# A unit of seven products and the plain unit beside it, matmul by matmul in turn

## The chip, the core and the metric

The kernel runs on one core of one Trainium2 chip. The metric is device time in microseconds, the median of several executions. Engines are named as in the profile: PE is TensorE (matmuls), PEld its loads of the stationary operand, ACT is ScalarE, DVE is VectorE, POOL is GpSimd, SP is SyncE, which issues the DMAs.

## What is computed

Two pre-norm residual layers of a decoder trunk, for 256 tokens of width 2048 in float32. Layer 0 mixes tokens with stick-breaking attention, layer 1 with a gated delta rule. Each is followed by a dense SwiGLU FFN with a hidden width of 5632:

```python
for i in range(DEPTH):
    h = rms_norm(x, mix_norm[i])
    y = stick_breaking_mixer(h, ...) if i == 0 else gated_deltanet_mixer(h, ...)
    x = x + y
    x = x + swiglu(rms_norm(x, ffn_norm[i]), ffn_w_gu[i], ffn_w_down[i])

def swiglu(h, w_gu, w_down):
    gate, up = jnp.split(h @ w_gu, 2, axis=-1)
    return (jax.nn.silu(gate) * up) @ w_down
```

The change concerns the FFNs alone.

## The kernel before

**Products.** A float32 product is made of three products of `fp32r` operands. Each operand is split into a high and a low part, and high x high, high x low and low x high are added up in PSUM. The activations are split once, when they are made. The weights come raw from memory and are split as they arrive: `convert` (L515) has ScalarE write the high part (`act`, L307) and VectorE the low part, the raw value minus the high one (`tt`, L311).

**Blocks and units.** A block is a product of all 256 tokens with 512 columns of a weight matrix. It is cut into units of two slices of 128 rows of the weights (`UK = 2`), and a unit is the step of the main loop. There are three lanes, each with its own buffers:

- a: outside the FFNs' middle; four pairs of high and low buffers.
- b: a plain unit inside the FFN. Two slices, two halves of the tokens and three products make 12 matmuls with 512 moving columns. Two raw buffers, two pairs of high and low buffers.
- s: a unit of seven products, for six of the eleven column blocks of gate and up. A product of 2 x 2 blocks is made with seven multiplications in place of eight, so there are 7 x 3 = 21 matmuls with 256 moving columns (`seven_products`, L582). The sums of weights that it needs are made first by VectorE (`sums`, L500: three operations), then converted: high part 128x1792, low part in one or two pieces. Two or three raw buffers, two pairs of high and low buffers.

A unit's high and low buffer goes back to its lane after its last matmul; its raw buffer goes back after its low part is made.

**The order of the work.** The kernel writes every engine's instructions itself, in one program order, with a small model of the engines' times (`spend`, L288). `ffn_units` (L821) and `merge` (L868) lay out the order of the s and b units: at most two s in a row, about 1.3 b to one s. A run of three or four b is common where a block of each ends.

`stream` (L620) goes through the units one by one. In each round it issues loads (`pump`, L477, on SP's queue), makes the sums of the s units up to three places on, and converts units while `ahead < i + AHEAD`, with `AHEAD = 3`, that is up to two places on. Then it writes the unit's matmuls (`product`, L543). Between groups of three matmuls `tick` (L267) lets waiting tasks go one step: evacuations of finished blocks (`quarters`, L1002, and others), transposes of hidden activations, norms. Their matmuls go into the same TensorE queue, their other steps into ScalarE's and VectorE's. An engine carries out its queue in program order.

Of the kernel before, what the change touches and what calls it, by code (L numbers as in the profile page):

```python
# [145 lines left out]
class Trunk:  # L146
# [393 lines left out]
        quarters = lambda *w: [q for a in w for q in self.cut(a, 256)]  # L540
        u.conv = (quarters(hi), quarters(*lo), end + HOP) if u.lane == "s" else (hi, lo[0], end + HOP)

    def product(self, u):  # L543
        b, (hi, lo, after) = u.block, u.conv
        ks = range(u.k0, u.k0 + u.nk)
        if b.kind == "ba":
            acc = b.acc[0]
            c = b.cols
            for k in ks:
                o = b.ops[k]  # L550
                wh, wl = hi[:, k * c:(k + 1) * c], lo[:, k * c:(k + 1) * c]
                for j, (w, x) in enumerate(((wh, o.hi), (wh, o.lo), (wl, o.hi))):
                    self.mm(acc[:c, :S], w, x, start=k == 0 and j == 0, stop=k == len(ks) - 1 and j == 2, after=after)
        elif b.kind == "seven":
            self.seven_products(u, hi, lo, after)
        else:
            for j, k in enumerate(ks):
                o = b.ops[k]
                if not o.ready:
                    self.until(lambda: o.ready, ("operand", b.name, k))  # L560
                self.tick()
                wh, wl = hi[:, j * NB:(j + 1) * NB], lo[:, j * NB:(j + 1) * NB]
                for t in range(NT):
                    if t:
                        self.tick()
                    a, sl = b.acc[t], slice(t * P, (t + 1) * P)
                    self.mm(a, o.hi[:, sl], wh, start=u.first and j == 0, stop=False, after=after)
                    self.mm(a, o.hi[:, sl], wl, start=False, stop=False)
                    self.mm(a, o.lo[:, sl], wh, start=False, stop=u.last and j == u.nk - 1)
                o.uses -= 1  # L570
                if o.uses == 0 and o.release:
                    o.release()
        u.done = True
        if u.lane == "a":
            self.freed.append(self.t["pe"])
        else:
            u.hibuf.t = self.t["pe"]
            self.lanes[u.lane][1].put(u.hibuf)
        if u.leaves:
            self.leave_b()  # L580

    def seven_products(self, u, hi, lo, after):  # L582


        b = u.block
        o = b.ops[u.k0 // 2]
        if not o.ready:
            self.until(lambda: o.ready, ("forms", b.name, u.k0))
        x = o.parts()

        for p, w, bank, half in ((1, 0, 1, 0), (2, 2, 0, 0), (4, 6, 3, 1), (3, 1, 3, 0), (5, 3, 2, 0), (7, 4, 2, 1), (6, 5, 0, 1)):
            self.tick()
            xh, xl = x[p - 1]
            a = b.acc[bank][:, 256 * half:256 * (half + 1)]
            self.mm(a, xh, hi[w], start=u.first and p in (1, 2, 4, 5), stop=False, after=after)
            self.mm(a, xh, lo[w], start=False, stop=False)
            self.mm(a, xl, hi[w], start=False, stop=u.last and p in (1, 6, 3, 7))
        o.uses -= 1

    def begin(self, b):  # L600
# [19 lines left out]
    def stream(self, units):  # L620
        self.units, self.at, self.freed, self.owner, self.more = units, 0, [], [None, None], None
        for i, u in enumerate(units):
            u.idx = i
            u.block.name = getattr(u.block, "name", i)
        for i in range(self.RAW):
            if i % 2 == 0:
                self.load_x(i // 2)
            self.load(units[i])
        self.load_x(3)
        self.spawn(self.more_constants(), "constants")  # L630
        ahead = 1
        self.convert(units[0])
        self.until(lambda: units[0].block.ops[0].ready, "first operand")
        for i, u in enumerate(units):
            self.at, spins = i, 0
            self.pump()
            while True:
                for v in units[i:i + self.AHEAD + 1]:
                    if v.lane == "s" and not v.summed:
                        if not v.loaded:  # L640
                            break
                        self.sums(v)
                while ahead < min(i + self.AHEAD, len(units)) and self.may_convert(units[ahead]):
                    self.convert(units[ahead])
                    ahead += 1
                    self.pump()
                if ahead > i:
                    break
                spins += 1
                assert spins < 100, ("conversion", u.block.name, u.lane, u.loaded)  # L650
                self.until(lambda: self.may_load(u) or u.loaded, ("load", u.block.name))
                self.pump()
            if u.first:
                self.begin(u.block)
            self.product(u)
            if u.last:
                b = u.block
                b.evacuated = False
                self.spawn(self.after_block(b), f"block {b.name}", front=True).urgent = True
        self.until(lambda: not self.tasks, "end")  # L660

    def load_x(self, n):

        self.nc.sync.dma_start(self.xs[n], self.ins["x"][0, :, n * NB:(n + 1) * NB].rearrange("(t p) d -> p t d", p=P))
        task = self.spawn(self.norm_part(self.norms[0], n), f"norm {n}")
        task.base = task.ready = self.transfer(P * NT * NB * 4, 0.0)
# [986 lines left out]
```

## Time and profile before

| | |
|---|---|
| median of 3 runs | 2745.24 us (2743.29 to 2746.49) |
| the profiled execution's own time | 2744.59 us |
| its span, first to last instruction | 2742.9 us |
| granted TensorE clock, mean | 0.998 |
| PE, PEld busy | 2706.2, 2305.9 us |
| DVE, ACT busy | 2169.5, 1489.6 us |
| read from HBM | 489.33 MB |
| units: lane a, b, s | 461, 260, 192 |
| stretches with s units | about 455 to 1052 and 2049 to 2645 us |

The page gives busy times and the busy share in 40 slices. The timeline lists instructions in order of time, with equal neighbours merged into one row (x2, x9): start, duration, engine, line, operation, `out<-in`, and in brackets the idle time before it with the engine that ended it. A matmul's duration in the rows is its way through the array, longer than the distance to the next start; that distance is its price. The windows view gives busy time by engine in a stretch, then the granted clock, the DMA share and GB/s. In the rows, b's raw and converted weights are `slab` and `slabs`, those of lanes s and a are `w`. Matmuls of s units have 256 moving columns and read `w`; those of b units have 512 and read `slabs`.

### The profile page before, as it was taken

Reading aid. Unit: us, or ns where it says so; the run is one execution under the profiler, and the core shown is the slowest. Engines: PE = TensorE matmul, PEld = TensorE weight load, DVE = VectorE, ACT = ScalarE, POOL = GpSimd, SP = SyncE. Lnnn points to the kernel's source line nnn. Section 1 sums busy time; section 2 is a strip of 40 time slices with the busy share of each in tenths; the row PEclk is TensorE's granted clock in tenths of the full one; section 3 lists DMA queues with packets and bytes.
Section 4 is the critical chain, followed back from the end, with each engine's and each line's share of the span. In section 5 each row is a group of like instructions: output and inputs, shape, how many; then the busy total and the mean of one; then the engine's idle time right before and its main releaser. Section 6 shows DMA issues by size and latency. Waiting matters only on the chain.

```text
span 2742.9 us, 39666 instructions
## 1 busy us (share of the span) xinstructions
PE 2706.2 (99%) x15018; PEld 2305.9 (84%) x15018; DVE 2169.5 (79%) x3378; ACT 1489.6 (54%) x1968; POOL 11.2 (0%) x95
## 2 busy tenths in 40 slices
PE   7999999999999999999999999999999999999999
PEld 6888888889888888888888888888878888888887
DVE  5555567899999897668878877987678899998975
ACT  5555555545554554555666556655565455455553
POOL 0000000000000000000000000000000000000000
PEclk9999999999999999999999999999999999999999
DMA  6555555656656656556655556556555566656564
GB/s 202 161 168 166 179 176 171 192 177 204 196 185 198 200 178 207 175 172 186 173 154 180 174 150 179 165 159 186 154 177 191 185 196 196 191 185 203 181 211 158
DMA packets 299835, 496.65 MB, mean 181 GB/s; under 512 B 37176, under 2 KB 79483, under 8 KB 299643
## 3 DMA queue, kind: packets, MB, share of 16 engines
q1 hardware_dynamic: 299594, 494.10, 57.8%
q8 instruction: 117, 1.92, 0.3%
q14 instruction: 76, 0.61, 0.1%
q10 hardware_dynamic: 48, 0.02, 0.0%
HBM read 489.33 MB, written 4.72 MB: 180 GB/s over the span
## 4 chain that ended last, share of the span: by engine, by line
PE 78%; DVE 14%; ACT 3%; issue 2%; DMA 2%; SPq 0%; ACTq 0%; DVEq 0%
PE acc L330 65%; PE bank L330 12%; DVE w L311 9%; DVE slabs L311 3%; PE bank L339 2%; ACT w L307 2%; DMA slab<-in_ffn_w_down_dram 1%; DVE slab L311 1%; DVE x L311 1%; ACT slab L307 0%; DMA slab<-in_ffn_w_gu_dram 0%; DVE slab L315 0%; DVE hTl L315 0%; DMA x<-in_x_dram 0%; ACT hTh L307 0%
## 5 line engine op out<-in xcount | busy, mean ns | idle before, releaser
L311 DVE TENSOR_TENSOR w<-w,w 128x1024 fp32r<-128x1024 f32 (+1 forms) x749 | 949.7, 1289 | 301.9 <-ACT w L307 297.3
L307 ACT ACTIVATE w<-w 128x1024 fp32r<-128x1024 f32 (+1 forms) x653 | 804.4, 1244 | 475.9 <-PE acc L330 272.5
L330 PE MATMUL acc<-w,hTh 128*128 128x512 f32 (+1 forms) x3296 | 948.6, 371 | 13.1 <-DVE w L311 7.9
L330 PEld LDWEIGHTS acc<-w,hTh 128*128 128x128 f32 x3296 | 594.4, 189 | 120.9 <-DVE w L311 12.9
L330 PE MATMUL acc<-w,hTl 128*128 128x512 f32 (+1 forms) x1648 | 603.8, 366 | 0.0
L307 ACT ACTIVATE slabs<-slab 128x1024 fp32r<-128x1024 f32 x260 | 272.3, 1052 | 320.4 <-PE acc L330 215.1
L311 DVE TENSOR_TENSOR slabs<-slab,slabs 128x1024 fp32r<-128x1024 f32 x260 | 315.6, 1219 | 68.7 <-ACT slabs L307 68.4
L330 PE MATMUL acc<-w,kh 128*128 128x512 f32 x1152 | 361.2, 395 | 0.0
L330 PEld LDWEIGHTS acc<-w,hTl 128*128 128x128 f32 x1648 | 311.5, 189 | 51.2
L330 PE MATMUL acc<-slabs,kh 128*128 128x512 f32 x1024 | 322.8, 394 | 5.9 <-DVE slabs L311 4.5
L330 PE MATMUL acc<-slabs,hTh 128*128 128x512 f32 x1056 | 328.1, 392 | 0.0
L311 DVE TENSOR_TENSOR w<-w 128x256 f32<-128x256 f32 (+1 forms) x576 | 293.7, 511 | 13.3
L330 PEld LDWEIGHTS acc<-w,kh 128*128 128x128 f32 x1152 | 211.6, 188 | 41.3
L330 PEld LDWEIGHTS acc<-slabs,kh 128*128 128x128 f32 x1024 | 187.6, 188 | 49.5 <-DVE slabs L311 11.8
L330 PEld LDWEIGHTS acc<-slabs,hTh 128*128 128x128 f32 x1056 | 193.4, 188 | 37.5 <-DVE slabs L311 1.1
L330 PE MATMUL acc<-w,kl 128*128 128x512 f32 x576 | 224.7, 390 | 0.0
L330 PE MATMUL acc<-slabs,hTl 128*128 128x512 f32 x528 | 205.6, 389 | 0.0
L330 PE MATMUL acc<-slabs,kl 128*128 128x512 f32 x512 | 199.7, 390 | 0.0
L330 PE MATMUL bank<-w,wide 128*128 128x256 f32 x1296 | 180.1, 284 | 0.0
L330 PEld LDWEIGHTS bank<-w,wide 128*128 128x128 f32 x1296 | 165.9, 192 | 0.0
L330 PEld LDWEIGHTS acc<-w,kl 128*128 128x128 f32 x576 | 108.1, 188 | 23.0
L330 PEld LDWEIGHTS acc<-slabs,hTl 128*128 128x128 f32 x528 | 99.2, 188 | 21.2
(203 smaller groups left out, 2378.1 us busy)
## 6 DMA issues: line engine op xcount, KB each, us to landing
w<-in_ffn_w_gu_dram SPq DMA_DIRECT2D x220, 512.0 KB, 4.1
slab<-in_ffn_w_gu_dram SPq DMA_DIRECT2D x132, 512.0 KB, 3.5
w<-in_gdn_w_in_dram SPq DMA_DIRECT2D x129, 512.0 KB, 3.9
slab<-in_ffn_w_down_dram SPq DMA_DIRECT2D x128, 512.0 KB, 4.4
w<-in_sb_w_in_dram SPq DMA_DIRECT2D x96, 512.0 KB, 3.6
w<-in_gdn_w_in_dram SPq DMA_DIRECT2D x128, 256.0 KB, 3.0
w<-in_gdn_w_out_dram SPq DMA_DIRECT2D x64, 512.0 KB, 3.8
w<-in_ffn_w_down_dram SPq DMA_DIRECT2D x48, 512.0 KB, 4.2
```

Source lines behind the costliest of these rows:

```text
L307: self.nc.scalar.activation(out, in_, func, **kw)
L311: self.nc.vector.tensor_tensor(out, a, b, op=op)
L330: self.nc.tensor.matmul(out, lhsT, rhs, start=start, stop=stop, skip_group_check=True)
L339: self.nc.tensor.transpose(out, in_, self.ident[:p, :p])
```

## The change

Two neighbouring units of which one is of lane s and the other of lane b are written together, unless the first ends its block or the second begins one. `product` becomes a generator, `products`, that stops after every matmul of an s or b unit, and `stream` takes one matmul from each of the two in turn until both are finished. The two must both be converted before the first matmul is written, and the loop then moves on by two units. `AHEAD` stays 3 and is counted from the first of the two. All other pairs of neighbours go as before. No instruction is added or removed; the tasks' `tick` calls stay where they are within each unit.

```diff
@@ seven_products and the plain branch of products, after each matmul
                     self.mm(a, o.hi[:, sl], wh, start=u.first and j == 0, stop=False, after=after)
+                    yield
                     self.mm(a, o.hi[:, sl], wl, start=False, stop=False)
+                    yield
                     self.mm(a, o.lo[:, sl], wh, start=False, stop=u.last and j == u.nk - 1)
+                    yield
@@ stream
-        for i, u in enumerate(units):
+        i = 0
+        while i < len(units):
+            u = units[i]
             self.at, spins = i, 0
+            both = self.together(*units[i:i + 2])
             self.pump()
...
-                if ahead > i:
+                if ahead > i + both:
                     break
                 spins += 1
                 assert spins < 100, ("conversion", u.block.name, u.lane, u.loaded)
-                self.until(lambda: self.may_load(u) or u.loaded, ("load", u.block.name))
+                v = units[ahead]
+                self.until(lambda: self.may_load(v) or v.loaded, ("load", u.block.name))
                 self.pump()
             if u.first:
                 self.begin(u.block)
-            self.product(u)
-            if u.last:
-                b = u.block
-                b.evacuated = False
-                self.spawn(self.after_block(b), f"block {b.name}", front=True).urgent = True
+            going = deque(self.products(v) for v in units[i:i + 1 + both])
+            while going:
+                try:
+                    next(going[0])
+                    going.rotate(-1)
+                except StopIteration:
+                    going.popleft()
+            for u in units[i:i + 1 + both]:
+                if u.last:
+                    b = u.block
+                    b.evacuated = False
+                    self.spawn(self.after_block(b), f"block {b.name}", front=True).urgent = True
+            i += 1 + both
+
+    def together(self, u, v=None):
+        return v is not None and {u.lane, v.lane} == {"s", "b"} and not u.last and not v.first
```

More of the change, by code (lines that the diff above doesn't have):

```diff
@@ L541, in convert, with products @@
         u.conv = (quarters(hi), quarters(*lo), end + HOP) if u.lane == "s" else (hi, lo[0], end + HOP)
-    def product(self, u):
+    def products(self, u):
         b, (hi, lo, after) = u.block, u.conv
@@ L554, in product @@
         elif b.kind == "seven":
-            self.seven_products(u, hi, lo, after)
+            yield from self.seven_products(u, hi, lo, after)
         else:
@@ L595, in seven_products @@
             self.mm(a, xh, hi[w], start=u.first and p in (1, 2, 4, 5), stop=False, after=after)
+            yield
             self.mm(a, xh, lo[w], start=False, stop=False)
+            yield
             self.mm(a, xl, hi[w], start=False, stop=u.last and p in (1, 6, 3, 7))
+            yield
         o.uses -= 1
```

## The prediction

> **What bounds the kernel now.** I read the page first (span, busy times, slices), then the windows of the two stretches that hold the units of seven products, then the waits of TensorE in them.
>
> ```profile
> span 2742.9 us, 39666 instructions
> ...
> PE 2706.2 (99%) x15018; PEld 2305.9 (84%) x15018; DVE 2169.5 (79%) x3378; ACT 1489.6 (54%) x1968; POOL 11.2 (0%) x95
> ...
> DVE  5555567899999897668878877987678899998975
> ```
>
> TensorE is the bound over the whole, and VectorE reaches nine tenths in slices 8 to 15 and again near the end. Those are the FFN stretches:
>
> ```profile
> 455.00:1052.00 597.00, 590.30 (x3543) 523.66 (x3542) 538.84 (x662) 308.54 (x268) 0.00 (x0) 1.00 0.60 192
> 2049.00:2645.00 596.00, 589.35 (x3539) 523.13 (x3538) 538.44 (x661) 307.68 (x267) 0.00 (x0) 1.00 0.60 192
> ```
>
> Columns are length, then busy time of PE, PEld, DVE, ACT, POOL. VectorE is busy for 90% of a stretch in which TensorE leaves only 6.7 us open. So two engines are nearly full, and the conversions on VectorE arrive just in time. What TensorE waited for in the first of the two:
>
> ```profile
> PE acc L330 <- DVE w L311: 3.7, 8, 0.9
> PE acc L330 <- DVE slabs L311: 2.2, 3, 1.4
> PE acc L330 <- ACT w L307: 0.6, 2, 0.4
> ```
>
> Thirteen waits, 6.5 us; the second stretch is alike. Today lateness costs almost nothing, because each unit is needed only when the one before it is finished.
>
> **How much of the kernel the change reaches.** From the units in their order, `together` takes neighbours of lanes s and b unless the first ends or the second begins a block. I wrote out that order: 82 pairs come of it (41 in each FFN; 66 with b first, 16 with s first), of 192 s units. 22 of the 82 follow directly on another pair. No instruction is added or removed; a pair is still 21 matmuls of 256 columns and 12 of 512. The first 24 of the 33 now alternate and the last nine are of 256.
>
> **The pace of alternating matmuls.** This is TensorE around one pair in its old order, s at 715.58 and b at 718.09:
>
> ```profile
> 714.22 0.62 PE L330 MATMUL acc<-slabs,kh 128*128 128x512 f32 x2
> 714.90 0.62 PE L330 MATMUL acc<-slabs,kh 128*128 128x512 f32 x2
> 715.35 0.39 PE L330 MATMUL acc<-slabs,kl 128*128 128x512 f32 x1
> 715.58 0.40 PE L330 MATMUL acc<-w,hTh 128*128 128x256 f32 x2
> 715.81 0.28 PE L330 MATMUL acc<-w,hTl 128*128 128x256 f32 x1
> 716.65 1.24 PE L330 MATMUL bank<-w,wide 128*128 128x256 f32 x9
> 717.73 0.52 PE L330 MATMUL acc<-w,wide 128*128 128x256 f32 x3
> 718.09 0.63 PE L330 MATMUL acc<-slabs,kh 128*128 128x512 f32 x2
> 718.56 0.39 PE L330 MATMUL acc<-slabs,kl 128*128 128x512 f32 x1
> ```
>
> The duration column holds the way through the array; the price of one is the distance between starts. Three of 512 columns from 714.22 to 714.90 make 0.227 each; nine of 256 from 716.65 to 717.73 make 0.120. Both are 13 ns above their columns at 2.4 per ns (213 and 107), so the extra is the same for either size. At the changes: the first two of 256 after a 512 take 715.81 - 715.58 = 0.23, 0.01 less than two steady ones; the first two of 512 after a 256 take 718.56 - 718.09 = 0.47, 0.016 more than two steady ones. The trace has no strict alternation, so I bound it. In the worst case each 512 behaves like the first two here (0.235) and each 256 gains nothing: 0.008 x 12 x 82 = +8 us. In the best case each 256 behaves as one that follows a 512 (the whole 0.01 falls on the first, 0.110) and the 512 loses nothing: -0.010 x 12 x 82 = -10 us. Added together the two observed ends nearly cancel (-0.01 and +0.016 per change), so I take 0.
>
> The Trainium skill, page "TensorE: Matmul & The Clock Gate", gives for the load of 128 stationary columns (section "LDWEIGHTS (loading the stationary operand)") 128/1.2 = 107 ns, and says in "Back-to-back issue gap" that both the load and the matmul set the spacing, with 256/2.4 + 2.5 = 109 ns for a matmul by itself. By that page a 256 run stands at its load's limit, a load would hide behind a 512, and 11 ns of 984 matmuls would go: an estimate of -11 us. The rows above speak against it: the 512s, long enough to hide any load, carry the same 13 ns.
>
> **What moves: when the second unit is needed.** TensorE starts its matmuls in the order of the code (the rows above), and the second matmul of the pair now belongs to the second unit. Its converted weights are needed 0.1 to 0.2 us after the first unit starts, not after that unit's 2.52 us (21 x 0.120) or 2.72 us (12 x 0.227). For the pair above:
>
> ```profile
> 714.12 1.05 ACT L307 ACTIVATE slabs<-slab 128x1024 fp32r<-128x1024 f32 x1
> 714.97 1.60 DVE L311 TENSOR_TENSOR w<-w 128x512 f32<-128x512 f32 x3
> 716.49 1.22 DVE L311 TENSOR_TENSOR slabs<-slab,slabs 128x1024 fp32r<-128x1024 f32 x1
> ```
>
> ScalarE has the high part of b at 715.17; VectorE first makes the sums of a later s unit and ends b's low part at 717.71. That is 2.13 us after s started and 0.38 before b needed it. In the new order TensorE stands for those 2.1 us, and its whole queue stands with it: the rest of the pair, the transposes and small products of the tasks that tick between, and through them ScalarE's evacuations. Reading all 82 pairs in this way (end of the second unit's last low part minus start of the first unit), the lateness is positive in every one: 0.10 to 3.90, mean 1.88, sum 154 us. The first and the last pair (0.10, the first of two low parts at 1.22 ending 460.88 against 460.78; and 2637.41 against 2636.46, 0.95):
>
> ```profile
> 460.78 0.40 PE L330 MATMUL acc<-w,hTh 128*128 128x256 f32 x2
> 459.66 2.35 DVE L311 TENSOR_TENSOR slabs<-slab,slabs 128x1024 fp32r<-128x1024 f32 x2
> 2636.46 0.63 PE L330 MATMUL acc<-slabs,hTh 128*128 128x512 f32 x2
> 2635.31 2.10 DVE L311 TENSOR_TENSOR w<-w,w 128x768 fp32r<-128x768 f32 x2 [0.64 <-ACT w L307]
> ```
>
> Not all of the 154 us is paid. Where VectorE's work runs on without a break, a wait of TensorE in one pair puts VectorE that much ahead for the next. Where a conversion has to wait for a buffer that TensorE gives back, the lead is lost. I followed each second unit's conversion back, operation by operation, to the matmul that released it, and took off the waits that earlier pairs had put in since. An example of a release:
>
> ```profile
> 480.38 1.06 ACT L307 ACTIVATE slabs<-slab 128x1024 fp32r<-128x1024 f32 x1 [0.80 <-PE acc L330]
> 481.34 1.69 ACT L307 ACTIVATE w<-w 128x1792 fp32r<-128x1792 f32 x1
> 483.06 2.03 DVE L311 TENSOR_TENSOR w<-w,w 128x1792 fp32r<-128x1792 f32 x1 [0.37 <-ACT w L307]
> 482.90 0.61 PE L330 MATMUL acc<-slabs,hTh 128*128 128x512 f32 x2
> ```
>
> The b lane has two pairs of high and low buffers, so the third b in a row converts only when the first is done (480.38); the s behind it is ready at 485.09, 2.19 after its partner b started at 482.90, and pays all of it. The two pairs right behind it have the same release and pay little. In all, 33 pairs pay 1.9 on average, 62 us, and the other 49 together 3: **+65 us**. Bounds: 154 if no lead is ever kept, 33 if half of these waits are covered as well.
>
> **Pairs right behind a pair.** `ahead` looks three units on from the first of a pair, so the second unit of the following pair is converted only in the following round, one unit later in the code than now. These are the durations that then stand in one line:
>
> ```profile
> L311 DVE TENSOR_TENSOR w<-w,w 128x1792 fp32r<-128x1792 f32 x144 | 196.4, 1398 | 22.3 <-ACT w L307 22.0
> L307 ACT ACTIVATE slabs<-slab 128x1024 fp32r<-128x1024 f32 x124 | 129.9, 1052 | 146.8 <-PE acc L330 87.5 <-DMA slab<-in_ffn_w_down_dram 34.4 <-DMA slab<-in_ffn_w_gu_dram 15.4
> L311 DVE TENSOR_TENSOR slabs<-slab,slabs 128x1024 fp32r<-128x1024 f32 x124 | 150.5, 1219 | 30.2 <-ACT slabs L307 30.1
> L311 DVE TENSOR_TENSOR w<-w 128x256 f32<-128x256 f32 (+1 forms) x282 | 143.9, 511 | 6.5
> ```
>
> High part of b 1.05, its low part 1.22, three sums of s 1.53, low parts of s 196.4/96 = 2.05: 5.85 us from the buffer's release, against 12 x 0.347 + 9 x 0.120 = 5.24 us of matmuls. That is 0.6 short before any hand-over between engines (the idle column gives 0.24 for one from ScalarE to VectorE). Also b's buffer comes free after 12 x 0.347 = 4.2 us and no longer after 2.7. I take 1.0 for each of the 22: **+22 us** (0 if the lead covers it, 45 at 2.05, a whole low part).
>
> **What is given back.** Of the 13 us that TensorE waits today in both stretches, some are absorbed by the new waits: **-6 us** (0 to -13). The raw loads are issued from the same queue in the same order, one round later behind a pair; loads wait for buffers that VectorE frees, so this adds nothing that isn't in VectorE's line above.
>
> **Clock.** One long wait lowers the granted clock (the figure after POOL):
>
> ```profile
> 43.00:46.00 3.00, 0.61 (x2) 0.54 (x3) 2.38 (x6) 1.36 (x3) 0.00 (x0) 0.50 0.85 283
> 46.00:50.00 4.00, 4.00 (x14) 3.12 (x13) 1.24 (x2) 0.00 (x0) 0.00 (x0) 0.55 0.48 146
> 2154.00:2157.00 3.00, 1.53 (x7) 0.98 (x6) 2.93 (x5) 2.44 (x3) 0.00 (x0) 1.00 0.00 0
> ```
>
> The 5 us wait before 45.39 brought it to 0.55 for the next 4 us, which costs 1.8; 1.5 us open near 2155 left it at 1.00. Most new waits are nearer to the latter, so 0 in the sum; four that are above 3 us could add 7. The skill's page named above, section "Why this matters for your kernels", puts the limit at idle gaps of about 3 us, which these rows allow.
>
> **Sum.** Against the profiled execution's own 2744.59 us (the span and 1.7 around it; the median of the runs is 0.65 above it): 0 + 65 + 22 - 6 = +81, so 2826 us. Low: 33 + 0 - 13 = +20, 2765. High: 154 + 22 - 6 = +170, 2915.
>
> **Rivals.**
> - *The lead is kept everywhere (no change).* If VectorE, once put ahead, stayed ahead, one wait of at most 3.9 us per FFN would do, less 6 given back: 2744.6 + 7.8 - 6 = 2746. For: it has 10% free. Against: the buffer releases above, which recur in each run of three b. Chance 0.07.
> - *Faster.* The new waits are covered and each 256 in turn sheds its 0.010: -10 us, 2735. It decides if the second unit is ready at the start in at least 70 of the 82 pairs, so that fewer than 10 us are lost. Against: 0 of 82 are ready in the trace. Chance 0.08. (By the page's load limit, weighed above, it would be -11 and 2734.)
> - *No lead is kept and clock drops join.* 154 + 45 + 7: about 2950. Chance 0.05.
> - *The forecast,* waits of 20 to 170 us: 0.80.
>
> A measurement of this kernel tells 0.2% (5.5 us) from no change. With the two slower cases: slower 0.85, within 0.2% 0.07, faster 0.08. The range 2765 to 2915 leaves out 0.2.
>
> **What would show it.** In the new profile TensorE's waits for VectorE ("w" and "slabs") should grow from 13 us to about 90 and its busy time in the two stretches stay near 1180 us, with the stretches longer by about 40 each; VectorE's share there falls from 90% to about 85%; the time outside stays within 2 us. Starts in a pair should lie 0.347 us apart from one 512 to the next. I am wrong if the waits stay under 20 us, or if 512 to 512 is off 0.347 by more than 0.01.

## The result, and the profile after

The changed kernel takes 2841.98 us (median of 5 runs, 2831.57 to 2843.57) against 2745.24 (5 runs of before): the ratio is 1.0345, with a 95% interval of 1.0334 to 1.0357. The prediction was 2826, slower.

The page's span and busy times, then the windows of the two FFN stretches (from the first unit before them to the last matmul; length, PE, PEld, DVE, ACT, POOL, clock, DMA share, GB/s):

```profile
span 2840.3 us, 39668 instructions
...
PE 2737.0 (96%) x15018; PEld 2318.2 (82%) x15018; DVE 2172.7 (76%) x3378; ACT 1489.4 (52%) x1968; POOL 11.3 (0%) x95
```

```profile
452.90:1109.50 656.60, 617.07 (x3601) 539.82 (x3600) 546.89 (x668) 312.39 (x272) 0.00 (x0) 0.98 0.56 176
2094.70:2749.60 654.90, 614.38 (x3601) 537.69 (x3600) 547.00 (x668) 312.21 (x272) 0.00 (x0) 0.99 0.56 176
```

The same units of the kernel before:

```profile
452.80:1059.30 606.50, 599.80 (x3602) 532.29 (x3601) 545.22 (x668) 312.64 (x272) 0.00 (x0) 1.00 0.60 191
2046.00:2652.20 606.20, 599.55 (x3601) 532.36 (x3600) 545.21 (x668) 312.58 (x272) 0.00 (x0) 1.00 0.60 191
```

The stretches are longer by 50.1 and 48.7 us; all the rest went from 1530.2 to 1528.8. VectorE and ScalarE do the same work as before (547 and 312 us) in more time. So nothing was added: TensorE stands. Its waits on conversions, over the whole span:

```profile
PE acc L330 <- DVE w L311: 55.4, 51, 3.1
PE acc L330 <- DVE slabs L311: 20.7, 16, 2.9
PE acc L330 <- ACT w L307: 3.4, 6, 1.1
```

Total, count and longest. 73 waits of 79.5 us stand where 27 of 13.6 us stood in the kernel before (7.9, 4.5 and 1.2 us in the same three rows). The prediction's pair, whose lateness was read as 2.13 us, now looks like this (TensorE, then VectorE):

```profile
733.55 0.28 PE L330 MATMUL acc<-w,hTh 128*128 128x256 f32 x1
733.66 0.40 PE L330 MATMUL acc<-slabs,kh 128*128 128x512 f32 x1
733.90 0.28 PE L330 MATMUL acc<-w,hTh 128*128 128x256 f32 x1
735.73 0.50 PE L330 MATMUL acc<-slabs,kh 128*128 128x512 f32 x1 [1.56 <-DVE slabs L311]
736.07 0.28 PE L330 MATMUL acc<-w,hTl 128*128 128x256 f32 x1
736.19 0.40 PE L330 MATMUL acc<-slabs,kl 128*128 128x512 f32 x1
```

```profile
732.94 1.60 DVE L311 TENSOR_TENSOR w<-w 128x512 f32<-128x512 f32 x3
734.46 1.22 DVE L311 TENSOR_TENSOR slabs<-slab,slabs 128x1024 fp32r<-128x1024 f32 x1
```

VectorE makes the sums of a later unit and then b's low part until 735.68, exactly as before: 2.13 us after s began at 733.55. TensorE gets through b's first matmul, which needs the high part alone, and stops at the second, which needs the low part. The row says 1.56 idle, but the start comes 1.83 after that of the matmul ahead of it, whose price is 0.12. So a wait costs 0.15 more than its row shows: a matmul's row lasts longer than the distance to the next start, and that overlap is lost too. With 46 more waits this makes some 7 us, an estimate from this one wait.

The clock fell as well:

```profile
core 0: 2840.3 us, clock 0.991
```

Before it was 0.998. The traces of both kernels record no other value than full and half. So 0.009 x 2 x 2840 = 51 us now run at half speed, and 0.002 x 2 x 2743 = 11 did before; half of the 40 us between them is lost time, **about 20 us**. The executions of the changed kernel bear this out: between the one at 0.995 (span 2829.8) and one at 0.991 (2841.2) lie 11.4 us, and 0.004 x 2840 is 11.4.

### The profile page after: what moved, and what is told of

It reads as the page before. It is cut to its first block, busy times and chain, and to the rows that moved or that the text cites. A ratio compares the mean times of both kernels' runs of the same rounds, so it can differ in the third digit from the quotient of the medians.

```text
span 2840.3 us, 39668 instructions
## 1 busy us (share of the span) xinstructions
PE 2737.0 (96%) x15018; PEld 2318.2 (82%) x15018; DVE 2172.7 (76%) x3378; ACT 1489.4 (52%) x1968; POOL 11.3 (0%) x95
## 4 chain that ended last, share of the span: by engine, by line
PE 78%; DVE 13%; ACT 5%; issue 3%; DMA 1%; SPq 0%; ACTq 0%; DVEq 0%
PE acc L330 64%; PE bank L330 12%; DVE w L311 9%; ACT w L307 4%; PE bank L339 2%; DVE slabs L311 2%; DVE x L311 1%; DMA slab<-in_ffn_w_down_dram 1%; ACT slab L307 1%; DVE slab L311 1%; DVE slab L315 0%; DVE hTl L315 0%; DMA x<-in_x_dram 0%; ACT hTh L307 0%; ACT slabs L307 0%
## 5 line engine op out<-in xcount | busy, mean ns | idle before, releaser
L330 PE MATMUL acc<-w,hTh 128*128 128x512 f32 (+1 forms) x3296 | 984.4, 373 | 63.8 <-DVE w L311 55.4
L330 PEld LDWEIGHTS acc<-w,hTh 128*128 128x128 f32 x3296 | 602.0, 190 | 183.4 <-DVE w L311 71.4
L330 PE MATMUL acc<-slabs,kh 128*128 128x512 f32 x1024 | 345.2, 402 | 17.5 <-DVE slabs L311 16.3
L330 PE MATMUL acc<-slabs,hTh 128*128 128x512 f32 x1056 | 356.3, 396 | 4.4 <-DVE slabs L311 4.4
L330 PEld LDWEIGHTS acc<-slabs,kh 128*128 128x128 f32 x1024 | 193.9, 193 | 60.3 <-DVE slabs L311 20.6
L330 PE MATMUL bank<-w,wide 128*128 128x256 f32 x1296 | 203.8, 283 | 0.0
L330 PEld LDWEIGHTS bank<-w,wide 128*128 128x128 f32 x1296 | 180.3, 191 | 3.0
```

What stands on the lines that cost most here:

```text
L330: self.nc.tensor.matmul(out, lhsT, rhs, start=start, stop=stop, skip_group_check=True)
```

## The experiments

Theory W: TensorE stands for the second unit's conversion, which the new order asks for earlier. Rival P: the change of size at every matmul costs. Rival O: the other order in which conversions are written, with the look-ahead, costs. Times are medians; the kernel before, run beside them, took 2744.89 in the first four and 2744.20 in the last three.

**The same pairs, matmuls not alternated.** Both units are still converted before the first matmul is written, and the loop still moves on by two.

```diff
-            while going:
-                try:
-                    next(going[0])
-                    going.rotate(-1)
-                except StopIteration:
-                    going.popleft()
+            for g in going:
+                for _ in g:
+                    pass
```

> The pair is kept in every respect but one: both units are converted before the first matmul is written and the loop moves on by two, but the first unit's matmuls are written out before the second's. Theory W (TensorE stands for the second unit's conversion, because its matmuls come early): the waits for VectorE in the two FFN stretches fall from 80 us back to 13 to 25, the clock stays above 0.995, time 2745 to 2765 us. Rival O (the other order of conversions and the look-ahead cost the time): stays at 2815 to 2842. Rival P (changing between 256 and 512 columns at every matmul is what costs): 2743 to 2760, like W; the next run parts these two.

2741.19 us, ratio 0.9988 (0.9979 to 0.9997): the loss is gone, with 3.7 us to the good. Its waits:

```profile
PE acc L330 <- DVE w L311: 6.0, 13, 0.9
PE acc L330 <- DVE slabs L311: 2.3, 6, 0.9
PE acc L330 <- ACT w L307: 1.2, 4, 0.4
```

9.5 us; the waits and the time both lie below their expected ranges. Rival O falls: it needs the loss in a kernel that has all of the bookkeeping.

**Early, but hardly alternated.** One matmul of the first unit, two of the second, then the first unit's rest, then the second's.

```diff
+            if both:
+                next(going[0])
+                next(going[1])
+                next(going[1])
-            while going:
...
+            for g in going:
+                for _ in g:
+                    pass
```

> Per pair: one matmul of the first unit, two of the second (its high and its low part), then the rest of the first, then the rest of the second. So two extra changes of size per pair in place of 24, but the second unit's weights are needed as early as in full alternation. Theory W: nearly the whole loss remains, waits 60 to 85 us, 2810 to 2845 us. Rival P (each change of size costs): 2 of 24 changes, 2745 to 2755 us. Rival O: 2815 to 2842 as well.

2820.95 us, ratio 1.028 (1.0264 to 1.0297), with a clock of 0.994:

```profile
PE acc L330 <- DVE w L311: 47.7, 39, 3.3
PE acc L330 <- DVE slabs L311: 19.5, 12, 3.0
PE acc L330 <- ACT w L307: 2.8, 6, 0.6
```

Two extra changes of size, where full alternation has 22 or 23 (the expectation says 24), keep 76 of the 97 us, and 70 of the 80 us of waits. Rival P falls: when the second unit is asked for decides, not how often the size changes.

**Conversions cut short, in order and alternated.** Two kernels, the one before and the changed one, in which after the first use of each buffer of lanes s and b only 64 columns of each part are made.

```diff
-        end = self.act(hi, src)
+        short = u.lane != "a" and getattr(u.hibuf, "seen", False)
+        if u.lane != "a":
+            u.hibuf.seen = True
+        end = self.act(hi[:, :64], src[:, :64]) if short else self.act(hi, src)
...
-            end = self.tt(a, src[:, n], hi[:, n].bitcast(F32), ALU.subtract)
+            m = slice(at, at + 64) if short else n
+            end = self.tt(a[:, :m.stop - m.start], src[:, m], hi[:, m].bitcast(F32), ALU.subtract)
```

> The kernel before, with conversions in lanes s and b cut short: after the first use of each buffer only 64 columns of the high part and of each low part are made, the rest keeps old values. That part of the computation is left out, so that VectorE and ScalarE are early. All theories: TensorE's 13 us of waits in the FFN stretches mostly go, 2720 to 2740 us. It is the base for the next run.

> The changed kernel with the same part of the conversions left out. Theory W: with the weights early, alternation by itself costs next to nothing: within -5 to +12 us of short_in_order, waits under 15 us, clock above 0.995. Rival P (the change of size at every matmul costs): +60 to +97 us against short_in_order, as in the full kernel. The load-limit rule, that a load hides behind the matmul of 512 columns: -11 us against short_in_order.

2718.52 us in order (slightly under the range expected) and 2725.23 alternated. With the weights early, alternation costs 6.7 us and no more; the other order of conversions is in this difference too. The alternated one's waits on conversions and its clock:

```profile
PE acc L330 <- DVE w L311: 0.6, 1, 0.6
```

```profile
core 0: 2722.0 us, clock 0.999
```

So the waits and the lower clock both go when the conversions are early. The 6.7 us fits the price of changing size; a stretch of this kernel's TensorE rows:

```profile
620.01 0.28 PE L330 MATMUL bank<-w,hTl 128*128 128x256 f32 x1
620.13 0.40 PE L330 MATMUL acc<-slabs,kl 128*128 128x512 f32 x1
620.37 0.28 PE L330 MATMUL bank<-w,wide 128*128 128x256 f32 x1
...
621.07 0.28 PE L330 MATMUL bank<-w,wide 128*128 128x256 f32 x1
621.19 0.40 PE L330 MATMUL acc<-slabs,kl 128*128 128x512 f32 x1
621.42 0.88 PE L330 MATMUL bank<-w,wide 128*128 128x256 f32 x6
```

From 620.01 to 621.07 there are three alternations, 0.353 each, against 0.347 in runs of one size: 0.006 x 984 = 6 us.

**Alternate only the last four matmuls of the first unit.**

```diff
+            if both:
+                for _ in range(17 if u.lane == "s" else 8):
+                    next(going[0])
             while going:
```

> Per pair the first unit goes alone until four of its matmuls are left (17 of 21, or 8 of 12), then the two alternate. The second unit's weights are needed 1.8 to 2.0 us later than in full alternation. Theory W: of the waits inside pairs, read from the changed kernel's trace pair by pair (54 pairs over 0.5 us, at most 3.5), only what lies above 1.9 us stays, some 10 to 25 us with what earlier waits no longer cover; 2750 to 2775 us, clock above 0.995. Rival O (order of conversions): about 2830. Rival P: a third of the alternations, a third of 97, about 2777.

2744.29 us, ratio 0.9999 (0.9989 to 1.0008), clock 0.998, waits:

```profile
PE acc L330 <- DVE w L311: 7.3, 10, 1.3
PE acc L330 <- DVE slabs L311: 3.7, 8, 0.8
PE acc L330 <- ACT w L307: 1.2, 4, 0.4
```

The second unit is asked for 1.8 to 2.0 us later and the whole loss goes, more than was expected: 12.2 us of waits are left, no more than before. A third of the alternations costs nothing that can be told.

**Look ahead from the second unit.**

```diff
-                for v in units[i:i + self.AHEAD + 1]:
+                for v in units[i:i + self.AHEAD + 1 + both]:
-                while ahead < min(i + self.AHEAD, len(units)) and self.may_convert(units[ahead]):
+                while ahead < min(i + self.AHEAD + both, len(units)) and self.may_convert(units[ahead]):
```

> The changed kernel with sums and conversions looked ahead from the second unit of a pair (one unit further). The prediction put 22 us on the 22 pairs right behind a pair, for conversions written one round late. If that term is right: 2815 to 2825 us. If the waits seen in those pairs (9 us in the changed kernel's trace) are all that hangs on it: 2830 to 2842.

2840.25 us, ratio 1.0351 (1.0337 to 1.0365), against 2841.98 for the changed kernel: nothing. The prediction's reason for its 22 us falls; conversions written a round earlier save no time.

**The same look-ahead without alternation.**

> Both units of a pair converted before the first matmul, matmuls in order, and sums and conversions looked ahead from the second unit. pair_in_sequence was 0.12 per cent under the kernel before. If earlier conversions of pairs save TensorE's small waits, 2735 to 2741 us; if that was all there was to have, 2740 to 2745.

2743.82 us, ratio 1.0000 (0.9991 to 1.0009). No gain. The 3.7 us of the first experiment isn't built upon in this way; its interval ends at 0.9997, so it is at the edge of what can be told, and no version was found that clearly beats the kernel before.

## Why the prediction was right, and where its sizes were off

**The mechanism held.** The second unit was late in the trace of before, the new order asked for it at once, and TensorE stood for it: shown by the waits in the trace, and by the loss, which disappears when the early need alone is taken away (pairs in sequence, late start), stays for the most part when the early need alone is left (early two), and disappears when the lateness is taken away (short conversions).

**Waits, +65 + 22 - 6 = 81.** In the rows the waits rose by 66 us (13.6 to 79.5); with the 7 us of overlap lost at their starts that is 73. The sum was near by luck, since two errors of opposite sign met in it. Pair by pair, as the distance between starts beyond the price, at full clock, the 60 pairs that don't follow another lost about 77 us and the 22 that do about 9. The term for pairs right behind a pair was too large, and its reason, the look-ahead, was refuted. The term for the rest was too small because I let VectorE keep leads that it lost. One place: the pair whose b begins at 797.33 (772.20 in the kernel before), where I had taken off all of its lateness; it lost 1.98 us. The conversion's own row on ScalarE, and the last matmul of the b two places ahead of it, whose high and low buffer it takes over, before:

```profile
768.76 0.39 PE L330 MATMUL acc<-slabs,kl 128*128 128x512 f32 x1
769.97 1.06 ACT L307 ACTIVATE slabs<-slab 128x1024 fp32r<-128x1024 f32 x1 [6.45 <-DMA slab<-in_ffn_w_down_dram]
```

and after, with the low part that gave its raw buffer back and the load into it:

```profile
789.06 1.22 DVE L311 TENSOR_TENSOR slabs<-slab,slabs 128x1024 fp32r<-128x1024 f32 x1
790.31 0.37 SPq L495 DMA_DIRECT2D slab<-in_ffn_w_down_dram  x1
793.90 0.40 PE L330 MATMUL acc<-slabs,kl 128*128 128x512 f32 x1
794.93 1.06 ACT L307 ACTIVATE slabs<-slab 128x1024 fp32r<-128x1024 f32 x1 [6.40 <-DMA slab<-in_ffn_w_down_dram]
795.89 1.69 ACT L307 ACTIVATE w<-w 128x1792 fp32r<-128x1792 f32 x1
```

Both times the conversion starts when its raw load has landed. That load was issued at 790.31, as soon as VectorE's low part (until 790.28) had freed the raw buffer, so "loads wait for buffers that VectorE frees" holds here. But a second condition stands close behind: the high and low buffer comes free with TensorE's last matmul on it, at 769.15 before (0.8 us ahead of the conversion) and at 794.30 after (0.6 us ahead). Whatever lead VectorE had, at most those 0.8 us of it could be used. So the step that failed is "I followed each second unit's conversion back, operation by operation, to the matmul that released it": as far as the traces tell, for this pair the condition that came last was followed to its end, and a lead also stops at the one that came next to last. Four pairs of the changed kernel (beginning at 522.06, 797.33, 859.14 and 2501.13) have such a load in front of their conversions and lost about 7 us together; there the buffer was free 0.4, 0.6, 0.4 and 2.0 us ahead of the conversion, so the loads themselves can account for 3.5 us at most. This is read from the traces; no run separates it.

**Pace, 0 (-10 to +8).** Measured +6.7. The bound from the two first matmuls after a change held, and its worse end was the nearer one. The Trainium skill's load limit, page "TensorE: Matmul & The Clock Gate", sections "LDWEIGHTS (loading the stationary operand)" and "Back-to-back issue gap", gave an estimate of -11 us; the two kernels with short conversions differ by +6.7, so it is wrong here.

**Clock, 0 (up to +7).** About 20, worked out above from the granted clock. The failing step was "Most new waits are nearer to the latter, so 0 in the sum": waits of 1.8 us were enough, as the last section shows.

**Sum.** 73 of waits and overlap, 20 of clock and 7 of pace are 100, against 97.4 between the two spans. The 4 us that pairing in sequence gains are no term of their own: its waits fell by the same 4 (13.6 to 9.5), and waits are counted already. The 16 us by which 2826 fell short are the clock's 20 and the pace's 7, less 8 by which the waits came out smaller; that is 19, and 3 stay unexplained.

**What the prediction said would show.** Waits "about 90" (79.5), VectorE's share "about 85%" (547/656, 83%), stretches longer "by about 40" (49) and the time outside within 2 us (1.4) held roughly. TensorE's busy time "near 1180" didn't: 1231, against 1199 for the same units before. The 32 us are roughly, by the estimates above, the clock's 20, since at half clock a matmul is counted busy for longer, the pace's 7 and the 7 of overlap, which the rows count as busy too. The start of one 512 to the next, 0.351 to 0.353, lay within 0.01 of 0.347.

## What to carry to other kernels

When two streams are merged on an in-order engine, the second stream's data is needed a whole unit earlier; before merging, compare when each operand is ready with the start of its partner, not with its own. The slack that a unit has today is its place in the queue, and a change that adds no instruction can spend it. To see how much of a lead an engine can keep, look at every condition that its next operation waits for, and not only at the one that came last. If the merge is wanted for another reason, let the second stream in late: the last four matmuls could be alternated here for nothing.

## What the runs showed of the hardware

The granted clock fell to half for 3.4 us after waits much shorter than the 5 us of the kernel before. (There, too, the clock was at half from 42.80 on, in the middle of that wait, which ends at 45.39.) The changed kernel's one wait ahead of 770.17, and the 512s behind it, now 0.64 apart in place of 0.35:

```profile
769.31 0.39 PE L330 MATMUL acc<-w,hTh 128*128 128x256 f32 x1 [1.83 <-DVE w L311]
...
770.26 0.63 PE L330 MATMUL acc<-slabs,kh 128*128 128x512 f32 x1
770.69 0.41 PE L330 MATMUL acc<-w,hTh 128*128 128x256 f32 x1
770.90 0.63 PE L330 MATMUL acc<-slabs,kl 128*128 128x512 f32 x1
```

A longer wait elsewhere did nothing:

```profile
2652.38 0.49 PE L330 MATMUL acc<-slabs,kh 128*128 128x512 f32 x1 [2.88 <-DVE slabs L311]
```

So the length of the wait alone doesn't decide. The trace shows what parts the two: all changes of the granted clock in it lie whole multiples of 3.413 us apart (from 579.02 to 647.29 there are 20 such steps, to 770.17 another 36). Windows cut at these steps:

```profile
766.76:770.17 3.41, 1.58 (x10) 1.13 (x9) 3.38 (x5) 2.65 (x2) 0.00 (x0) 1.00 0.24 90
770.17:773.58 3.41, 3.41 (x13) 2.93 (x12) 2.27 (x3) 0.00 (x0) 0.00 (x0) 0.50 0.89 294
2647.51:2650.92 3.41, 1.99 (x10) 1.43 (x8) 3.34 (x6) 0.00 (x0) 0.00 (x0) 1.00 0.82 259
2650.92:2654.33 3.41, 1.95 (x13) 1.74 (x14) 3.34 (x6) 2.30 (x2) 0.00 (x0) 1.00 0.33 90
2654.33:2657.74 3.41, 3.41 (x25) 3.09 (x24) 2.12 (x3) 0.47 (x1) 0.00 (x0) 1.00 0.77 249
```

The 1.83 us lie within one step, and the next runs at half clock. The 2.88 us are cut into 1.42 and 1.46, and nothing follows. In the two FFN stretches the clock fell eleven times, each time behind a step with 1.79 us or more of idleness; one further step, with 1.80 us from 2685.05, had no drop behind it, nor had any with 1.56 or less. The border isn't sharp across kernels: with the look-ahead from the second unit one drop came behind 1.49 us. And idleness isn't all of it: the kernel before drops once behind a step without any, in which some of the matmuls are small (32x32, or one column):

```profile
1571.98:1575.39 3.41, 3.41 (x47) 2.55 (x46) 3.41 (x6) 1.44 (x3) 0.00 (x0) 1.00 0.32 86
1575.39:1578.80 3.41, 3.41 (x9) 2.64 (x10) 1.57 (x10) 3.25 (x9) 0.00 (x0) 0.50 0.65 209
```

That a wait's place against these steps decides would also explain the scatter of the five executions (0.991 to 0.995); no run here tested it. The Trainium skill, page "TensorE: Matmul & The Clock Gate", section "Why this matters for your kernels", names gaps of about 3 us; the trace has drops after 1.8.

A matmul of 128 stationary columns and `fp32r` operands takes its columns at 2.4 per ns plus 13 ns, with 256 and with 512 columns alike: 0.120 and 0.227 from start to start, so 256 more columns take 107 ns, and 13 are left over at either size. At a change of size the 256 gains 3 and the 512 loses about 9 ns (means of 0.117 and 0.236 in the alternated kernel with short conversions). So a strict alternation is dearer by 6 ns than two runs.
